# Splitting weights ahead of the two phase changes, rows of tile 1 lagging behind tile 0, gates and reloads of x moved to other queues, and a reordered opening

## The chip, the cores and the metric

The kernel runs on one core of a Trainium2 chip. The metric is the device time of one execution in microseconds (us). TensorE (PE) multiplies, VectorE (DVE) and ScalarE (ACT) do elementwise work, GpSimd (POOL) does a few one-column operations, and SyncE (SP) issues the loads. Each engine works through its own list in order; an instruction that waits holds up everything behind it on its engine.

## The reference

One encoder layer on 256 rows of width 2048 in float32, with three residual steps, each between a modulated norm in front and a gated norm behind:

```python
mod = (c_act @ w_ada[l] + b_ada[l]).reshape(bsz, N_MOD, D_MODEL)[:, :, None, :]
...
h = modulate(rms_norm(x, ffn1_pre_g[l]), sh1, sc1)
y = swiglu(h, ffn1_w_gu[l], ffn1_w_down[l])
x = x + 0.5 * gt1 * rms_norm(y, ffn1_post_g[l])
h = modulate(rms_norm(x, mix_pre_g[l]), sh2, sc2)
proj = h @ w_in[l]
...
y = merged @ w_out[l]
x = x + gt2 * rms_norm(y, mix_post_g[l])
h = modulate(rms_norm(x, ffn2_pre_g[l]), sh3, sc3)
y = swiglu(h, ffn2_w_gu[l], ffn2_w_down[l])
x = x + 0.5 * gt3 * rms_norm(y, ffn2_post_g[l])
```

The middle step turns `proj` into attention heads and a gated block-mixing part, which are normed and joined as `merged`. The hidden width of the two SwiGLU steps is 5504.

## The kernel before

The 256 rows are two tiles of 128, t0 and t1, and the depth of 2048 is 16 blocks of 128 called kt. Every weight is used once for both tiles. Products are made to float32 accuracy with three matmuls of 128x128 by 128x512: the stationary operand and the weight are each split into a coarse part (hi) and a rest (lo), and `mm3` (L106 to L108) adds hi by hi, hi by lo and lo by hi. A weight goes through four steps: a 1 MB load `raw` on SP's queue (L112, three buffers), two casts `hi` on ACT (L144), two subtractions `lo` on DVE (L145), and the matmuls. The pairs `hi`, `lo` stand in slots, 4 from the pool `wsp` and, in some stages, 3 more.

The stages, with the times at which the profiled execution passes them: the opening up to 22 us (norm of x, its transposes `xtp`, the first modulation vectors, and the first split weights); FFN1 up to 747 (gate and up projections `gu`, then down projections `dn`); the in-projections `pj`, attention and gating, up to about 1016; the out-projection `wo` up to 1105; FFN2 up to the end. The modulation vectors come from 144 blocks `ada` of 1 MB, each reduced by one DVE operation (L191) and spread over the program by `tick`, a counter with a rate per visit of a weight.

Two places are called phase changes here. Phase change 1 lies between FFN1's `dn` and the first `pj`, phase change 2 between `wo` and FFN2's first `gu`. At each the kernel has to finish a residual step and begin the next one, for t0 and then for t1: add the last bank of the product to `y` (L428 or L905), square and sum it on ACT (L160), get the reciprocal root `r` with a sum `ms` on DVE (L165) and a power on POOL (L167), multiply by the gate row (L277), update x by `r` (L288, four pieces), square and sum x, get a second `r` in the same way, scale x by it (`xn`, L254), transpose (`xtp`, L257, PE), apply gain and shift while copying out of PSUM (`h`, L264 on ACT and L266 on DVE), and split (`hhi` L244, `hlo` L245). Only then do the matmuls of the next product have an operand.

What stands around that in each engine's list is decided by a scheduler that takes the order of the code, with a higher priority for the phase changes' own steps; `order["split"]` ties the first splits of the next product behind the steps of t0. The first weights of the next product are therefore split among the steps of the change. Inside `in_pair` (L655) and `ffn`, t0 and t1 use each kt in turn; only the second half of `wo` lets t1 lag by 6 kt. The gate row is a column that PE transposes, ACT copies, and two DMAs on SP's queue store to memory (`gd`, L234) and load as a row for all partitions (`gate`, L236). Before phase change 2, x is loaded back from memory on SP's queue (L84).

The opening is written out by hand as two chains, one for ACT and one for DVE (L610 to L616), that are prolonged by the first splits (L474).

## Time and profile before

| | us |
|---|---|
| median of 3 runs | 1850.29 (1850.15 to 1850.95) |
| the profiled execution | 1849.47 |
| its span, first to last instruction | 1847.7 |
| PE busy | 1802.8 |
| DVE busy | 1336.7 |
| ACT busy | 856.2 |
| POOL busy | 29.7 |

The mean granted clock of PE is 0.987 of full speed. A row of the timeline gives start, duration, engine, line, operation and tiles, and in brackets the idle time before it with what ended it. The duration that the profile gives a matmul (0.39 us) is longer than the distance at which matmuls follow each other, since they overlap in the array; a count of starts is the better measure of PE's work. A row of the windows gives, for one stretch, each engine's busy time and instructions, then the granted clock, the busy share of the DMA engines and their GB/s. A row of the waits names who waited for what, the sum, the number of times, and the longest.

### The profile page before, as it was taken

How to read it: one execution, taken by the hardware profiler on the slowest of the kernel's cores; microseconds unless marked ns; L12 is line 12 of the kernel's file. 1: busy time of each engine (PE TensorE's matmuls, PEld its weight loads, DVE VectorE, ACT ScalarE, POOL GpSimd, SP SyncE). 2: the span in 40 equal slices, each digit the busy share in tenths (PEclk: the TensorE clock that was granted, in tenths of full speed). 3: DMA queues.
4: the chain of work that ended last, by engine and by line, in shares of the span. 5: the costliest groups of instructions: out<-in, count | busy, mean ns of one | idle time of the engine just before them, and what ended most of it. 6: DMA issues, size and time to landing. Idle time of an engine off the chain costs nothing. (4 is left out here: it accounts for less than half of the span.)

```text
span 1847.7 us, 21177 instructions
## 1 busy us (share of the span) xinstructions
PE 1802.8 (98%) x8207; PEld 1494.5 (81%) x8207; DVE 1336.7 (72%) x1491; ACT 856.2 (46%) x1105; POOL 29.7 (2%) x54
## 2 busy tenths in 40 slices
PE   7999999999999999899999998999999999999997
PEld 6777788888888898688878876888888888888896
DVE  6989998987878865987889968774445555445455
ACT  6544355454344343745555556444444443443442
POOL 0000000000000000000001100000000000000000
PEclk8999999999999999899999998999999999999999
DMA  8988788988888875588878975885555555555462
GB/s 353 420 335 317 287 321 335 332 330 335 323 325 343 316 275 199 197 326 318 319 300 316 348 278 217 329 320 203 183 187 201 183 193 193 185 199 186 159 247 72
DMA packets 71478, 499.11 MB, mean 270 GB/s; under 512 B 7968, under 2 KB 8144, under 8 KB 13136
## 3 DMA queue, kind: packets, MB, share of 16 engines
q1 hardware_dynamic: 71376, 497.75, 71.6%
q8 instruction: 64, 1.05, 0.2%
q14 instruction: 38, 0.31, 0.0%
HBM read 493.50 MB, written 4.22 MB: 269 GB/s over the span
## 5 line engine op out<-in xcount | busy, mean ns | idle before, releaser
L145 DVE TENSOR_TENSOR lo<-raw,hi 128x1024 fp32r<-128x1024 f32 (+1 forms) x636 | 762.1, 1209 | 444.1 <-ACT hi L144 442.7
L144 ACT CAST hi<-raw 128x1024 fp32r<-128x1024 f32 (+1 forms) x636 | 658.1, 1043 | 883.8 <-PE gu L108 491.4
L106 PE MATMUL gu<-hi,hhi 128*128 128x512 f32 (+1 forms) x1408 | 542.6, 388 | 9.3 <-DVE acc L344 4.2
L107 PE MATMUL gu<-lo,hhi 128*128 128x512 f32 (+1 forms) x1408 | 543.1, 386 | 5.5 <-DVE lo L145 5.5
L108 PE MATMUL gu<-hi,hlo 128*128 128x512 f32 (+1 forms) x1408 | 542.5, 385 | 0.0
L191 DVE CUSTOM_DVE_ANT_0 ada<-ada,c_bc,small 128x2048 f32<-128x2048 f32 x144 | 337.3, 2344 | 9.3 <-DMA ada<-in_w_ada_dram 9.2
L106 PEld LDWEIGHTS gu<-hi,hhi 128*128 128x128 f32 x1408 | 265.6, 189 | 63.4 <-ACT hi L144 5.1
L107 PEld LDWEIGHTS gu<-lo,hhi 128*128 128x128 f32 x1408 | 265.3, 188 | 56.6 <-DVE lo L145 7.3
L108 PEld LDWEIGHTS gu<-hi,hlo 128*128 128x128 f32 x1408 | 265.1, 188 | 50.3 <-DVE hlo L245 0.3
L106 PE MATMUL dn<-hi,ah 128*128 128x512 f32 x640 | 249.2, 389 | 0.0
L107 PE MATMUL dn<-lo,ah 128*128 128x512 f32 x640 | 249.0, 389 | 0.0
L108 PE MATMUL dn<-hi,al 128*128 128x512 f32 x640 | 249.0, 389 | 0.0
L106 PEld LDWEIGHTS dn<-hi,ah 128*128 128x128 f32 x640 | 120.1, 188 | 25.0
L107 PEld LDWEIGHTS dn<-lo,ah 128*128 128x128 f32 x640 | 120.2, 188 | 24.9
L108 PEld LDWEIGHTS dn<-hi,al 128*128 128x128 f32 x640 | 120.1, 188 | 24.9
L107 PE MATMUL pj<-lo,hhi 128*128 128x512 f32 x320 | 127.7, 399 | 5.5 <-DVE lo L145 5.4
L106 PE MATMUL pj<-hi,hhi 128*128 128x512 f32 x320 | 128.2, 401 | 0.4 <-ACT hhi L244 0.4
L108 PE MATMUL pj<-hi,hlo 128*128 128x512 f32 x320 | 127.1, 398 | 0.0
L107 PEld LDWEIGHTS pj<-lo,hhi 128*128 128x128 f32 x320 | 60.7, 190 | 18.7 <-DVE lo L145 7.6
L106 PEld LDWEIGHTS pj<-hi,hhi 128*128 128x128 f32 x320 | 60.8, 190 | 12.3 <-ACT hhi L244 0.9
L108 PEld LDWEIGHTS pj<-hi,hlo 128*128 128x128 f32 x320 | 60.7, 190 | 11.6
L167 POOL TENSOR_TENSOR r<-ms,mhalf 128x1 f32<-128x1 f32 x16 | 21.4, 1335 | 1583.5 <-DVE ms L165 1583.5
(145 smaller groups left out, 1014.2 us busy)
## 6 DMA issues: line engine op xcount, KB each, us to landing
raw<-in_w_gu_dram SPq DMA_DIRECT2D x158, 1024.0 KB, 4.8
ada<-in_w_ada_dram SPq DMA_DIRECT2D x144, 1024.0 KB, 6.9
raw<-in_w_dn_dram SPq DMA_DIRECT2D x86, 1024.0 KB, 4.8
raw<-in_w_in_dram SPq DMA_DIRECT2D x40, 1024.0 KB, 5.0
raw<-in_w_out_dram SPq DMA_DIRECT2D x16, 1024.0 KB, 4.9
raw<-in_w_gu_dram SPq DMA_DIRECT2D x16, 768.0 KB, 4.3
x<-in_x_dram SPq DMA_DIRECT2D x4, 1024.0 KB, 7.4
...
```

What stands on the lines that cost most here:

```text
L106: nc.tensor.matmul(ps, ah, wh, start=start, stop=False)
L107: nc.tensor.matmul(ps, ah, wl, start=False, stop=False)
L108: nc.tensor.matmul(ps, al, wh, start=False, stop=stop)
L144: i_hi = nc.scalar.copy(hi[:, :n], raw)
L145: i_lo = nc.vector.tensor_tensor(lo[:, :n], raw, hi[:, :n].bitcast(F32), op=ALU.subtract)
L167: nc.gpsimd.tensor_tensor(r, ms, mhalf, op=ALU.pow)
L191: inst = nc.vector.tensor_tensor_reduce(out=st, in0=st, in1=c_bc, scale=1.0, scalar=bada[:, i:i + 1], op0=ALU.mult, op1=ALU.add, accum_out ...
```

## The change

The number of large matmuls stays, and so do the loads of weights. Seven things are new.

- **Splits ahead at phase change 1.** `down_last` calls `ahead1` after its own weights: three visits of `w_in` (6 kt) are loaded and split before t0's last banks are read out, into slots that now also come from the two `ada` buffers and a new pool. `in_pair(sp=sp1, lag=8)` uses them; t0 runs ahead, and t1 follows 8 kt behind.
- **Splits ahead at phase change 2.** The first three visits of FFN2's `w_gu2` are loaded and split in the second half of `wo` (one half-visit after it), and FFN2's first chunk is a `lead_chunk` with the same lag of 8. The second half of `wo` no longer lags by 6: t0 does kt 0 to 3 and then bank by bank kt 4 to 7, and t1 the same after it.
- **The scaling of x by `r`.** In `pre`, the four DVE operations `xn` of 128x512 per tile are gone. One DVE operation makes `dg`, the identity times `r`, and PE multiplies x by `dg` in plain float32 where it transposed `xn`.
- **Gates and reloads of x.** The store `gd` goes on ACT's queue and the load `gate` on GpSimd's, and both are put off by two ticks; the reload of x before phase change 2 goes on GpSimd's queue, earlier. The second gate is made inside the last `out_pair`.
- **The opening.** Both tiles' sums of squares are shared between ACT and DVE; three of four copies of `c_bc` are on ACT; of t1's four scalings one is on DVE; and the cast `hi` of the second weight stands ahead of three late copies of `xnT`.
- **Slots** are taken from sequences that `use_slots` writes down for each stage.
- **The rate** of `ada` blocks in FFN1 is 0.77 instead of 0.7.

The core of the diff:

```diff
+    def use_slots(*parts, once=()):
+        flat = lambda ps: [p for p, n in ps for _ in range(n)]
+        slots["seq"] = itertools.chain(flat(once), itertools.cycle(flat(parts)))
+    def slot():
+        pool = next(slots["seq"])
+        if pool is adap:
+            st = adap.tile([P, D], F32R, tag="ada", name=nm("adas"))
+            return st[:, :1024], st[:, 1024:]
...
+        if later:
+            step = later.pop(0)
+            if step:
+                step()
...
-        row = sm.tile([KT, P], F32, tag="xn", name=nm("grow"), bufs=2)
-        nc.scalar.copy(row, ps)
-        gd = dr.tile([KT, P], F32, tag=f"gd{i}", name=nm("gd"))
-        nc.sync.dma_start(gd, row)
-        g = gp.tile([P, D], F32, tag="gate", name=nm("gate"))
-        nc.sync.dma_start(g, gd[:, :].rearrange("k p -> (k p)").partition_broadcast(P))
-        return g
+        res = []
+        def spread():
+            row = sm.tile([KT, P], F32, tag="xn", name=nm("grow"), bufs=2)
+            inst = nc.scalar.copy(row, ps)
+            after(inst, order["last"][0])
+            gd = dr.tile([KT, P], F32, tag=f"gd{i}", name=nm("gd"))
+            nc.scalar.dma_start(gd, row)
+            g = gp.tile([P, D], F32, tag="gate", name=nm("gate"))
+            nc.gpsimd.dma_start(g, gd[:, :].rearrange("k p -> (k p)").partition_broadcast(P))
+            res.append(g)
+        later.extend([None, spread])
+        return res
...
+        dg = sm.tile([P, P], F32, tag="xn", name=nm("dg"), bufs=2)
+        nc.vector.tensor_scalar(dg, ident, r, None, op0=ALU.mult)
         for j in range(4):
-            xn = sm.tile([P, CH], F32, tag="xn", name=nm("xn"), bufs=2)
-            nc.vector.tensor_scalar(xn, x[t][:, j * CH:(j + 1) * CH], r, None, op0=ALU.mult)
             ps = ptr.tile([P, 4, P], F32, tag="tr", name=nm("xtp"))
             for q in range(4):
-                nc.tensor.transpose(ps[:, q, :], xn[:, q * P:(q + 1) * P], ident)
+                nc.tensor.matmul(ps[:, q, :], x[t][:, (4 * j + q) * P:(4 * j + q + 1) * P], dg, start=True, stop=True)
...
+        def lead_chunk(c, sp):
+            w = CHUNKS[c][1]
+            ps_of[c] = banks()
+            sp = list(sp)
+            def mm(kt, t):
+                for b in range(2):
+                    mv = (sp[kt][0][:, b * w:(b + 1) * w], sp[kt][1][:, b * w:(b + 1) * w])
+                    mm3(ps_of[c][b][t][:, :w], hst(kt, t), mv, kt == 0, kt == KT - 1)
+            for kt in range(KT + LEAD):
+                if kt < KT and kt >= len(sp):
+                    raw = gu_load(c, kt // 2)
+                    sp += [split(raw[:, 2 * q * w:2 * (q + 1) * w]) for q in range(2)]
+                if kt < KT:
+                    mm(kt, 0)
+                if kt >= LEAD:
+                    mm(kt - LEAD, 1)
...
+            if not tail:
+                ahead()
...
-            chain(first_act, hi0, h0[0], h0[1], late_evac[0], late_evac[1], late_evac[2], hi1, hi2, h1[0], h1[1], hi3)
+            chain(first_act, hi0, h0[0], h0[1], hi1, late_evac[0], late_evac[1], late_evac[2], hi2, h1[0], h1[1], hi3)
...
+            if lead and c == 0:
+                lead_chunk(0, lead)
+                use_slots(*after_lead)
+                p0 = pe
...
-    xn1 = on_act[-4:]
-    first_act = chain(*on_act[:-4], xn1[0], xn1[1], i_evac[0, 0], i_evac[0, 1], xn1[2], xn1[3],
-                      i_evac[0, 2], i_evac[0, 3], i_evac[1, 0])
+    first_act = chain(i_silu, sq_act[0], *i_c[1:], sq_act[1], i_evac[0, 0], i_evac[0, 1],
+                      i_xn[1, 1], i_xn[1, 2], i_xn[1, 3], i_evac[0, 2], i_evac[0, 3], i_evac[1, 0])
     late_evac = [i_evac[1, j] for j in range(1, 4)]
-    first_dve = chain(*on_dve)
+    first_dve = chain(i_c[0], sq_dve[0], i_ms[0], i_xn[0, 0], i_xn[0, 1], sq_dve[1], i_ms[1],
+                      i_xn[0, 2], i_xn[0, 3], i_xn[1, 0])
...
+        def ahead1():
+            ahs.close()
+            pre = wx.enter_context(tc.tile_pool(name="pre1", bufs=2))
+            rest = ((adap, 2), (pre, 2), (wsp, 4), (wx1, 3))
+            use_slots(*rest, once=((wx1, 1),) + rest)
+            for _ in range(3):
+                sp1.extend(in_visit())
...
-        ffn(a["w_gu1"], a["w_dn1"], h, ap_, PLAN, 0.7, gate1, finish1)
+        ffn(a["w_gu1"], a["w_dn1"], h, avp, ahp, PLAN, 0.77, gate1, finish1, ahead=ahead1)
...
+        for kt in range(KT + lag):
+            if kt < KT and kt >= len(sp):
+                sp += in_visit()
+            for b in range(2):
+                if kt < KT:
+                    mm(kt, 0, b)
+                if kt >= lag:
+                    mm(kt - lag, 1, b)
...
-    pa = in_pair()
+    pa = in_pair(sp=sp1, lag=LEAD)
     tick_acc[1] = 0.9
-    slots["extra"] = None
+    use_slots((wsp, 1))
...
+        def gate2():
+            flush_ada(GT[1])
+            gain(2, 0, KT)
+            g.append(gate(1, 1.0, gp))
+        ps = out_pair(m_b, [gate2])
...
+        use_slots((adap, 1), once=((wsp, 3), (wx2, 3), (wsp, 1)))
+        sp = wo_visit() + wo_visit()
         for t in range(NT):
             for b in range(2):
-                evac_b(t, b, ps[b][t])
-        LAG = 6
+                evac_b(t, b, ps[b][t], order["last"])
+        x2.extend(load_x(x_dram, nc.gpsimd))
         ps = wo_banks()
-        sp = []
-        for kt in range(8 + LAG):
-            if kt < 8 and kt % 2 == 0:
-                sp += wo_visit()
-            if kt < 8:
-                wo_mm(ps, m_b, sp[kt], kt, 0)
-            if kt >= LAG:
-                wo_mm(ps, m_b, sp[kt - LAG], kt - LAG, 1)
+        for kt in range(4):
+            wo_mm(ps, m_b, sp[kt], kt, 0)
+        sp += wo_visit() + wo_visit()
+        for b in range(2):
+            for kt in range(4, 8):
+                wo_mm(ps, m_b, sp[kt], kt, 0, (b,))
+        use_slots((wsp, 1), once=((adap, 1), (wsp, 4)))
+        sp3 = []
+        for p in range(3):
+            raw = load(a["w_gu2"], p * P * 2048, 2048)
+            sp3.append((raw, [split(raw[:, 1024 * q:1024 * (q + 1)]) for q in range(2 if p < 2 else 1)]))
+        for kt in range(4):
+            wo_mm(ps, m_b, sp[kt], kt, 1)
+        for b in range(2):
+            for kt in range(4, 8):
+                wo_mm(ps, m_b, sp[kt], kt, 1, (b,))
...
+        lead = [sl for _, sls in sp3 for sl in sls] + [split(raw[:, 1024:])]
```

On DVE at phase change 1, before (`y_395` and `y_396` are t0's and t1's sums, `dn_5559` t0's last bank, `dn_5577` to `dn_5597` t1's first three, `ms_5572` and `ms_5633` the two sums of squares of t0):

```order
L428 TENSOR_TENSOR y_395_2045<-y_395_2045,dn_5559 128x512
L165 TENSOR_REDUCE ms_5572<-ysq_5483 128x1
L277 TENSOR_TENSOR y_395_2045<-y_395_2045,gate_5177 128x512
L288 SCALAR_TENSOR_TENSOR x_969_5162<-y_395_2045,r_5574,x_969_5162 128x512 x4
L428 TENSOR_TENSOR y_396_2046<-y_396_2046,dn_5577 128x512
L428 TENSOR_TENSOR y_396_2046<-y_396_2046,dn_5587 128x512
L165 TENSOR_REDUCE ms_5633<-xsq_5619 128x1
L428 TENSOR_TENSOR y_396_2046<-y_396_2046,dn_5597 128x512
L254 TENSOR_SCALAR xn_5637<-x_969_5162,r_5635 128x512
```

and now, with `y_392` and `y_393` for t0 and t1, `dn_5610` t0's last bank and `dn_5628` to `dn_5648` t1's first three:

```order
L479 TENSOR_TENSOR y_392_2049<-y_392_2049,dn_5610 128x512
L479 TENSOR_TENSOR y_393_2050<-y_393_2050,dn_5628 128x512
L176 TENSOR_REDUCE ms_5623<-ysq_5502 128x1
L303 TENSOR_TENSOR y_392_2049<-y_392_2049,gate_5234 128x512
L314 SCALAR_TENSOR_TENSOR x_972_5184<-y_392_2049,r_5625,x_972_5184 128x512 x4
L303 TENSOR_TENSOR y_393_2050<-y_393_2050,gate_5234 128x512
L479 TENSOR_TENSOR y_393_2050<-y_393_2050,dn_5638 128x512
L479 TENSOR_TENSOR y_393_2050<-y_393_2050,dn_5648 128x512
L176 TENSOR_REDUCE ms_5684<-xsq_5670 128x1
L156 TENSOR_TENSOR lo_5543<-raw_5540,hi_5542 128x1024
L277 TENSOR_SCALAR dg_5688<-ident,r_5686 128x128
```

The add of t1's first bank stands ahead of t0's first `ms` where it stood behind the updates of x; a gate multiplication of t1 and two adds stand ahead of the second `ms`, and a split of weights (`lo_5543`) between it and `dg`, where the first `xn` was.

On PE at the same place, before, from t0's third group of transposes (`waits` names the engines whose signal an instruction waits for):

```order
L257 MATMUL xtp_5667<-ident,xn_5665 128x128 [waits DVE_49,Activation_49]
L257 MATMUL xtp_5667<-ident,xn_5665 128x128 x3
L106 MATMUL pj_5791<-hi_5797,hhi_5617 128x512 [waits Activation_49]
L257 MATMUL xtp_5681<-ident,xn_5679 128x128 [waits DVE_49,Activation_49]
L257 MATMUL xtp_5681<-ident,xn_5679 128x128 x3
L107 MATMUL pj_5791<-lo_5798,hhi_5617 128x512 [waits DVE_49]
L108 MATMUL pj_5791<-hi_5797,hlo_5618 128x512
L106 MATMUL pj_5791<-hi_5813,hhi_5617 128x512
L107 MATMUL pj_5791<-lo_5814,hhi_5617 128x512 [waits DVE_49]
L108 MATMUL pj_5791<-hi_5813,hlo_5618 128x512
```

and now:

```order
L281 MATMUL xtp_5714<-dg_5688,x_972_5184 128x128 [waits DVE_49,Activation_49]
L281 MATMUL xtp_5714<-dg_5688,x_972_5184 128x128 x3
L113 MATMUL pj_5828<-hi_5542,hhi_5668 128x512 [waits Activation_49]
L114 MATMUL pj_5828<-lo_5543,hhi_5668 128x512
L113 MATMUL pj_5830<-hi_5542,hhi_5668 128x512
L114 MATMUL pj_5830<-lo_5543,hhi_5668 128x512
L281 MATMUL xtp_5726<-dg_5688,x_972_5184 128x128 [waits DVE_49,Activation_49]
L281 MATMUL xtp_5726<-dg_5688,x_972_5184 128x128 x3
L115 MATMUL pj_5828<-hi_5542,hlo_5669 128x512 [waits DVE_49]
L115 MATMUL pj_5830<-hi_5542,hlo_5669 128x512
L113 MATMUL pj_5828<-adas_5546,hhi_5668 128x512
L114 MATMUL pj_5828<-adas_5546,hhi_5668 128x512
```

Each `lo` used to carry a wait for DVE; now the waits on this stretch are for `hhi`, `hlo` and the copies out of PSUM, and the weights of the next kt (`adas_5546`) carry none.

On PE at phase change 2, before, from t0's third group of transposes:

```order
L257 MATMUL xtp_8686<-ident,xn_8684 128x128 [waits DVE_49,Activation_49]
L257 MATMUL xtp_8686<-ident,xn_8684 128x128 x3
L106 MATMUL wo_8487<-hi_8560,mb_7491 128x512
L107 MATMUL wo_8487<-lo_8561,mb_7491 128x512
L108 MATMUL wo_8487<-hi_8560,mb_7492 128x512
L106 MATMUL gu_8810<-hi_8816,hhi_8624 128x512 [waits Activation_49]
L257 MATMUL xtp_8700<-ident,xn_8698 128x128 [waits DVE_49,Activation_49]
L257 MATMUL xtp_8700<-ident,xn_8698 128x128 x3
L107 MATMUL gu_8810<-lo_8817,hhi_8624 128x512
L108 MATMUL gu_8810<-hi_8816,hlo_8625 128x512 [waits DVE_49]
L106 MATMUL gu_8810<-hi_8820,hhi_8624 128x512
L107 MATMUL gu_8810<-lo_8821,hhi_8624 128x512
```

and now, from the last matmul of `wo`:

```order
L115 MATMUL wo_8512<-adas_8553,mb_7500 128x512
L281 MATMUL xtp_8687<-dg_8685,x_1657_8505 128x128 [waits DMASW1_49,DVE_49]
L281 MATMUL xtp_8687<-dg_8685,x_1657_8505 128x128 x3
L281 MATMUL xtp_8699<-dg_8685,x_1657_8505 128x128 x4
L281 MATMUL xtp_8711<-dg_8685,x_1657_8505 128x128 [waits DVE_49,Activation_49]
L281 MATMUL xtp_8711<-dg_8685,x_1657_8505 128x128 x3
L113 MATMUL gu_8834<-adas_8582,hhi_8653 128x512 [waits Activation_49]
L114 MATMUL gu_8834<-adas_8582,hhi_8653 128x512
L113 MATMUL gu_8836<-adas_8582,hhi_8653 128x512
L281 MATMUL xtp_8723<-dg_8685,x_1657_8505 128x128 [waits DVE_49,Activation_49]
L281 MATMUL xtp_8723<-dg_8685,x_1657_8505 128x128 x3
L115 MATMUL gu_8834<-adas_8582,hlo_8654 128x512 [waits DVE_49]
```

Matmuls of `wo` for t1 used to stand between the groups of transposes; now they all stand ahead of the first one.

On ACT in the opening, before:

```order
L160 ACTIVATE junk_144,xsq_153<-x_2_91 128x2048
L600 ACTIVATE xn_188<-x_2_91,r_158 128x512
L600 ACTIVATE xn_195<-x_2_91,r_158 128x512
L611 COPY xnT_216<-xtp_162 128x4x128
L611 COPY xnT_216<-xtp_169 128x4x128
L600 ACTIVATE xn_202<-x_2_91,r_158 128x512
L600 ACTIVATE xn_209<-x_2_91,r_158 128x512
L611 COPY xnT_217<-xtp_176 128x4x128
L611 COPY xnT_217<-xtp_183 128x4x128
L611 COPY xnT_216<-xtp_190 128x4x128
L144 CAST hi_239<-raw_226 128x1024
L625 ACTIVATE h_42_243<-xnT_216,mod,gmul 128x256
```

and now:

```order
L171 ACTIVATE junk_144,xsq_153<-x_2_91 128x1024
L667 COPY xnT_214<-xtp_164 128x4x128
L667 COPY xnT_214<-xtp_171 128x4x128
L656 ACTIVATE xn_18_161<-x_2_91,r_159 128x512 x3
L667 COPY xnT_215<-xtp_178 128x4x128
L667 COPY xnT_215<-xtp_185 128x4x128
L667 COPY xnT_214<-xtp_191 128x4x128
L155 CAST hi_237<-raw_224 128x1024
L681 ACTIVATE h_39_241<-xnT_214,mod,gmul 128x256
L268 CAST hhi_112<-h_39_241 128x256
L155 CAST hi_245<-raw_226 128x1024
L667 COPY xnT_214<-xtp_197 128x4x128
```

The square of x's second tile covers half the width, one of four scalings (`xn`) is gone from the list, the first `xnT` copies stand ahead of the scalings, and the second weight's cast (`hi_245`, before `hi_247`) follows `hhi` directly, ahead of three copies.

More of the change, by code (lines that the diff above doesn't have):

```diff
@@ L627, in h_first, with in_visit @@
         return (i_h,) + split_act(h32, h[0][:, kt, :], h[1][:, kt, :])
+    win_off = [0]
+    def in_visit():
+        raw = load(a["w_in"], win_off[0], 2048)
+        win_off[0] += P * 2048
+        tick()
+        return [split(raw[:, 1024 * q:1024 * (q + 1)]) for q in range(2)]
     PLAN = []
@@ L913, in block_kernel @@
-        ps = out_pair(m_b)
-        x2.extend(load_x(x_dram))
+            inst = nc.vector.scalar_tensor_tensor(out=y[t][:, ns], in0=ps, scalar=rb[t], in1=y[t][:, ns], op0=ALU.mult, op1=ALU.add)
+            if behind:
+                after(inst, behind[1])
+            return y_done(t, n, y, ysq, g, sm.tile([P, CH], F32, tag="xn", name=nm("junk"), bufs=2), behind)
+        use_slots((wsp, 4), (wx2, 3))
+        g = []
+        def gate2():
+            flush_ada(GT[1])
+            gain(2, 0, KT)
+            g.append(gate(1, 1.0, gp))
```

156 lines of the change are left out of this document (79 added, 77 removed).

## The prediction

> **What bounds the kernel now.** I read the page's engine rows and its groups first, then PE's timeline where it waits.
>
> ```profile
> PE 1802.8 (98%) x8207; PEld 1494.5 (81%) x8207; DVE 1336.7 (72%) x1491; ACT 856.2 (46%) x1105; POOL 29.7 (2%) x54
> ```
>
> ```profile
> L145 DVE TENSOR_TENSOR lo<-raw,hi 128x1024 fp32r<-128x1024 f32 (+1 forms) x636 | 762.1, 1209 | 444.1 <-ACT hi L144 442.7
> ```
>
> PE is busy for 98% of the span, and the large matmuls stay as many, so a gain can only come from the stretches where PE waits or runs at a lower clock. DVE splits the weights in 636 operations of 1.21 us, and PE's two longest waits after the opening are for such a `lo`. The timeline of PE shows them, first at phase change 1, then at phase change 2:
>
> ```profile
> 746.93 1.06 PE L257 MATMUL xtp<-ident,xn 128*128 128x128 f32 x8 [0.42 <-DVE xn L254]
> 749.95 0.66 PE L257 MATMUL xtp<-ident,xn 128*128 128x128 f32 x4 [1.95 <-ACT h L264]
> ...
> 759.63 0.80 PE L107 MATMUL pj<-lo,hhi 128*128 128x512 f32 x1 [5.17 <-DVE lo L145]
> ```
>
> ```profile
> 1106.91 1.09 PE L257 MATMUL xtp<-ident,xn 128*128 128x128 f32 x8 [1.45 <-DVE xn L254]
> 1107.76 0.48 PE L108 MATMUL wo<-hi,mb 128*128 128x512 f32 x1
> ...
> 1122.19 0.80 PE L107 MATMUL gu<-lo,hhi 128*128 128x512 f32 x1 [3.51 <-DVE lo L145]
> ```
>
> What each change costs in all is a count. Eight transposes take 0.85 us (1106.91 to 1107.76), 0.106 each. The distance of large matmuls is read in `wo`, beside a product in plain float32 (`zp`) that I need below:
>
> ```profile
> 1021.00 1.95 PE L844 MATMUL zp<-uv,wst 128*128 128x128 f32 x16
> 1022.70 0.48 PE L106 MATMUL wo<-hi,ma 128*128 128x512 f32 x1
> ...
> 1023.25 0.39 PE L108 MATMUL wo<-hi,ma 128*128 128x512 f32 x1
> ...
> 1028.01 0.39 PE L108 MATMUL wo<-hi,ma 128*128 128x512 f32 x1
> ```
>
> From 1023.25 to 1028.01 there are 21 steps, 0.227 each. Now the windows that hold the two changes, for PE whole, and for `xtp` alone:
>
> ```profile
> 746.10:769.30 23.20, 14.61 (x56) 9.59 (x55) 21.77 (x39) 19.80 (x46) 2.56 (x5) 0.71 0.42 163
> 1105.00:1128.80 23.80, 14.78 (x65) 10.68 (x64) 21.47 (x37) 20.02 (x44) 2.92 (x4) 0.78 0.30 111
> ```
>
> ```profile
> 746.10:769.30 23.20, 5.87 (x32) 4.49 (x32) 2.67 (x7) 7.07 (x18) 0.71 0.42 163
> 1105.00:1128.80 23.80, 4.92 (x28) 3.84 (x28) 2.34 (x6) 6.90 (x18) 0.78 0.30 111
> ```
>
> Phase change 1 holds 56 - 32 = 24 large matmuls and 32 transposes: 24 x 0.227 + 32 x 0.106 = 8.8 us of work in 23.2, a loss of 14.4. Phase change 2 holds 37 and 28: 11.4 of 23.8, a loss of 12.4. Part of the loss is clock, 0.71 and 0.78 on average:
>
> ```profile
> 748.20:751.60 3.40, 1.24 (x6) 0.69 (x7) 3.40 (x9) 3.40 (x9) 0.00 (x0) 1.00 0.00 0
> 1113.40:1116.80 3.40, 0.90 (x3) 0.30 (x2) 3.38 (x7) 3.40 (x12) 0.10 (x1) 1.00 0.49 207
> 215.70:219.10 3.40, 1.60 (x6) 1.05 (x6) 3.40 (x6) 1.27 (x2) 0.00 (x0) 1.00 0.44 183
> 752.00:765.00 13.00, 7.53 (x21) 4.72 (x20) 12.12 (x20) 9.93 (x22) 2.39 (x4) 0.50 0.45 166
> ```
>
> After 3.4 us with PE busy for 1.24, the clock was 0.50 for 13 us; after 0.90 it fell as well; after 1.60 it did not.
>
> **Phase change 1.** The splits ahead remove the wait of 5.17 us and those after it: kt 0 to 5 are split before, and 6 kt of t0 alone are 36 matmuls, 8.2 us of work that needs no split. What is late next is the chain to the second `r`. Its old course on DVE:
>
> ```profile
> 738.81 0.68 DVE L428 TENSOR_TENSOR y<-y,dn 128x512 f32<-128x512 f32 x1
> 740.34 0.16 DVE L165 TENSOR_REDUCE ms<-ysq 128x1 f32<-128x5 f32 x1 [0.85 <-ACT junk L160]
> ...
> 745.39 0.15 DVE L165 TENSOR_REDUCE ms<-xsq 128x1 f32<-128x5 f32 x1
> 745.46 0.68 DVE L428 TENSOR_TENSOR y<-y,dn 128x512 f32<-128x512 f32 x1
> 746.30 0.88 DVE L254 TENSOR_SCALAR xn<-x,r 128x512 f32<-128x512 f32 x2 [0.16 <-POOL r L167]
> ```
>
> An ACT cast of the splits ahead now stands before the cast of `aw` and waits for PE; I put 0.55 us of idle PE on it, about half a cast (2.01 for two in a row quoted below; bounds 0 and 1.1). The add of t1's first bank moves ahead of t0's first `ms`. That bank ends 9 matmuls, 2.04 us, after t0's last, so with the 0.55 the add ends near 742.0 where `ms` began at 740.34: the chain is 1.7 us later. The updates follow as before, but a gate multiplication (as long as the add, 0.68) comes ahead of the second `ms`, which so begins at 745.39 + 1.7 + 0.68 = 747.8, and a split of 1.2 us and the end of POOL's power stand between `ms` and `dg`. That gives `dg` at 749.5 against the end of `dn` at 746.93 - 0.42 + 0.55 = 747.05, and PE idle for 2.1 to 2.7 us where it was 0.42; I take 2.4, the middle. The third group of products waits until the first is copied out: 1.95 above, and less now that no cast stands ahead of that copy on ACT, so between 0 and 1.95; I take 0.75. The first `pj` waits for `hhi` and the first `hlo` product again, 0.45 together by the 0.20 to 0.25 that one signal takes. Then t1: DVE has 21 operations between the two `dg`, about 14 us at 0.4 to 1.2 each with two POOL waits, and PE 16 products and 36 matmuls, 11.6 us, and the 1.2 us of waits just named; I get 1.0 (0 to 2). Sum of idle: 0.55 + 2.4 + 0.75 + 0.45 + 1.0 = 5.15.
>
> The products with `dg` are plain float32 matmuls. The 16 records of `zp` are 8 products in 1.70 us, 0.213 each: 32 x (0.213 - 0.106) = 3.4 us of PE more. The four removed `xn` save DVE 1.8 us per tile, which lie beside other work. So the loss becomes 8.55 instead of 14.4: **5.85 gained**.
>
> **Phase change 2.** `wo` for t1 now ends before the first product, and the chain's last add, that of t1's final bank, stands ahead of `dg` and waits for PE's last `wo`. That add (some 0.7), POOL's power, `dg` and the signals between them make PE wait 1.6 to 2.4 us where it waited 1.45 and then had `wo` to do; I take 2.1, nearer to the upper end, since a cast stands ahead of the last squares on ACT. The copy of the first group costs 1.1, since a split stands ahead of it on DVE, `hhi` 0.2, t1's `dg` 1.2 (0 to 2). That is 4.6, and 3.4 for float32: 8.0 instead of 12.4, **4.4 gained**.
>
> **The opening.**
>
> ```profile
> 21.80 1.22 PE L106 MATMUL gu<-hi,hhi 128*128 128x512 f32 x2 [2.15 <-ACT hhi L244]
> 31.16 0.50 PE L106 MATMUL gu<-hi,hhi 128*128 128x512 f32 x1 [0.76 <-ACT hhi L244]
> ```
>
> ```profile
> 23.09 2.01 ACT L144 CAST hi<-raw 128x1024 fp32r<-128x1024 f32 x2
> 30.07 0.60 ACT L625 ACTIVATE h<-xnT,mod,gmul 128x256 f32<-128x256 f32 x1 [4.96 <-DVE gmul L203]
> ```
>
> ```profile
> 20.00:30.00 10.00, 8.20 (x23) 6.50 (x24) 7.37 (x9) 5.07 (x8) 0.00 (x0) 0.60 0.83 347
> 30.00:40.00 10.00, 9.24 (x41) 7.25 (x40) 9.44 (x11) 8.40 (x13) 0.00 (x0) 1.00 0.79 304
> 60.00:70.00 10.00, 10.00 (x45) 7.94 (x43) 9.96 (x11) 5.18 (x8) 0.00 (x0) 1.00 1.02 428
> ```
>
> Adding up ACT's list in its new order, `hhi` comes near 17 to 18 instead of 21.8, about 4 us earlier; the second cast (23.09) stands in front of the late copies, so the second pair of `ada` and with it the next `h` (30.07) come 5 to 6 us earlier. But the loads are the limit soon after: the DMA engines are full at 60 to 70, and what they have free is 0.17 and 0.21 of two windows, 3.8 us. I take **3.5 gained** (1.5 to 5.5). The rate of 0.77 moves `ada` blocks to where DVE still has idle time, and I cost it at nothing.
>
> **Sum.** 5.85 + 4.4 + 3.5 = 13.75 from 1849.47 gives 1835.7; the runs' median lies 0.8 above the profiled execution, so 1836.5.
>
> **Gate and clock, against the Trainium skill.**
>
> ```profile
> L167 POOL TENSOR_TENSOR r<-ms,mhalf x16: 550/928/2591, 9.0 to 1840.0; 128x1 f32<-128x1 f32 x16
> ```
>
> ```profile
> DMA to landing us min/median/max: 6.8/7.4/8.2
> ```
>
> The second gate is the tight one. It is put off to the third of four visits of the last `out_pair`, 2 x 24 x 0.227 = 10.9 us into it. Splits run about a visit (5.4) ahead of PE; with 7.4 us for the load and as much again for the store before it, it lands at 10.9 - 5.4 + 14.8 = 20.3. It is needed when the pair (21.8 us) and four adds are done, at 24.5: some 4 us to spare. The reload of x goes out ahead of it on the same queue and is needed a half `wo` later (24 x 2 x 0.227 = 10.9 us), and gates 1 and 3 have a whole `dn` between load and use; with that cover I cost them at nothing, and without it they would stop DVE in the same way. The slots only say where a split is kept: at nothing too, as long as no split waits for a slot that PE still reads, and then for at most that kt's 12 matmuls, 2.7 us. In these rows a one-column POOL operation takes 0.55 us at best and 2.59 beside a busy DVE, 4.7 times as long.
> The Trainium skill (SBUF — State Buffer, "SBUF: two separate sides") says that a DMA from GpSimd's queue has its descriptors written by GpSimd, which some VectorE operations lock out; a 620 ns transfer became 3100, and by that factor of 5 the estimate for this gate is 37 us. The rows of POOL agree in kind; no load on that queue is in this trace.
>
> On the clock, the skill (TensorE: Matmul & The Clock Gate, "HAM oscillation") has the abstract rule "no PE-idle gaps >~3.4µs". By it the longest new gap, 2.7, would keep the clock, and the first rival below would have no chance. The trace differs: the longest single gap in the 3.4 us before 751.6 was 1.95, and the clock fell, so the rows decide.
>
> **The rivals.**
> - *The clock falls again* at one or both changes. A gap of 2.1 to 2.4 leaves PE at most 1.3 of 3.4 us if it lies within one such stretch (between 1.24, which fell, and 1.60, which did not), more if it is shared by two. Two to three stretches at half clock cost 3.4 to 5.1: 1840 for one, 1844 for both. Chance 0.27.
> - *The opening is hidden* by full DMA engines: 1836.5 + 3 = 1839.5. For it speaks 1.02 at 60 to 70. Chance 0.09.
> - *The phases gain little*, because the chain to `dg`, and not the splits, sets them: t1's `dg` comes 3 us later at each, 1842.5 for both. For it speaks how many operations remain between; chance 0.08.
> - *Slower: the second gate lands late.* DVE stops at the first multiplication, and behind it in its list stand all splits of the second half of `wo`, so PE stops too. At 7.4 x 4.7 = 35 us it is 27.6 later, less 4 to spare: 1836.5 + 23.4 = 1860. The change turns slower from a load of about 26 us on. Against it: POOL does little else, and only the issuing could stretch. Chance 0.06.
>
> The forecast itself has 0.50. If every gap is at its lower bound (0.55 + 0.3 + 0.75 + 1.0 less at the first change, 0.5 + 1.2 at the second) and the opening gives 5.5, it is 1830.2; with one fall of the clock at 5.1 and an opening of 1.5 it is 1843.6. The range, rounded outward, is 1829 to 1844. About 0.2% (3.7 us) is what a measurement can tell from no change: all cases but the last lie below 1846.6, and I leave 0.06 for two falls of the clock together with a poor opening. Faster 0.88, same 0.06, slower 0.06.
>
> **What would show it.** Right: no wait of PE for `lo` at either change, one gap of 2 to 3 us ahead of each first `xtp`, product records at 0.106 two by two, the clock at 1.00 through both, the first `gu` near 18. Wrong: a clock of 0.50 after a change; DVE waiting for the gate's DMA; a long gap before t1's products; PE waiting for `hi` or `lo` between 30 and 90.

## The result, and the profile after

The changed kernel takes 1839.39 us (median of 4 runs, 1838.25 to 1840.22) where the kernel before, run beside it, takes 1850.62. The ratio is 0.9935, with a 95% interval from 0.9923 to 0.9946: 11 us faster. The forecast was 1836.5, in a range of 1829 to 1844. The profiled execution took 1839.32 us, 10.15 less than the one of before, with a span of 1837.2. One execution of experiment eight took 2600.89 us at a granted clock of 0.654, a slow state, and is not in its median below.

The page's row of the engines, and two rows of PE's waits (sum, number, longest):

```profile
PE 1803.2 (98%) x8271; PEld 1501.1 (82%) x8271; DVE 1328.4 (72%) x1481; ACT 854.5 (47%) x1105; POOL 31.3 (2%) x59
```

```profile
PE dn L113 <- ACT aw L424: 1.1, 2, 0.9
...
PE gu L114 <- DVE lo L156: 0.3, 1, 0.3
```

PE has 64 records more (8271 against 8207), the second halves of the 64 products with `dg`. Its waits for `lo`, which held the two longest before, are down to one of 0.3 us, in the opening. PE's timeline at phase change 1, then at phase change 2:

```profile
748.30 4.73 PE L281 MATMUL xtp<-dg,x 128*128 128x128 f32 x24 [2.30 <-issue]
...
763.09 2.02 PE L281 MATMUL xtp<-dg,x 128*128 128x128 f32 x16 [0.81 <-ACT hi L155]
```

```profile
1104.32 2.05 PE L281 MATMUL xtp<-dg,x 128*128 128x128 f32 x16 [1.77 <-DVE dg L277]
1107.57 1.16 PE L281 MATMUL xtp<-dg,x 128*128 128x128 f32 x8 [1.20 <-ACT h L288]
...
1116.59 2.02 PE L281 MATMUL xtp<-dg,x 128*128 128x128 f32 x16 [0.58 <-ACT hi L155]
```

One gap stands ahead of each first product, 2.30 and 1.77 us, and short ones later. The row of the first names no releaser; DVE's timeline has it:

```profile
746.19 0.15 DVE L176 TENSOR_REDUCE ms<-xsq 128x1 f32<-128x5 f32 x1
746.26 1.21 DVE L156 TENSOR_TENSOR lo<-raw,hi 128x1024 fp32r<-128x1024 f32 x1
747.91 0.28 DVE L277 TENSOR_SCALAR dg<-ident,r 128x128 f32<-128x128 f32 x1 [0.44 <-POOL r L178]
```

A split of 1.21 us stands between the second sum and `dg`, as the prediction had it, and `dg` ends at 748.19, 0.1 before the first product. The count that the prediction made of before is made here again: windows around the two changes, for PE whole, then for `xtp` alone.

```profile
745.60:769.50 23.90, 20.79 (x115) 17.63 (x113) 19.39 (x34) 19.51 (x45) 3.00 (x6) 0.93 0.56 215
1102.10:1123.60 21.50, 17.95 (x109) 15.24 (x109) 19.99 (x34) 21.01 (x48) 2.08 (x4) 1.00 0.46 160
```

```profile
745.60:769.50 23.90, 9.85 (x64) 9.20 (x64) 2.77 (x7) 7.58 (x20) 0.93 0.56 215
1102.10:1123.60 21.50, 8.39 (x64) 7.78 (x64) 2.85 (x7) 7.93 (x21) 1.00 0.46 160
```

Phase change 1 holds 115 - 64 = 51 large matmuls and 64 records of products: 51 x 0.227 + 64 x 0.106 = 18.4 us of work in 23.9, 5.5 lost. The second halves of the products, 32 x 0.106 = 3.4, are work that before did not have, and ahead of the window PE waits for `aw`, 1.1 us in all where the waits of before have 0.5:

```profile
PE dn L106 <- ACT aw L376: 0.5, 2, 0.2
```

That is 5.5 + 3.4 + 0.6 = 9.5 against 14.4 of before: 4.9 gained. Phase change 2 holds 45 and 64: 17.0 of 21.5, 4.5 lost, 7.9 with the 3.4, against 12.4: 4.5 gained. The clock at phase change 1:

```profile
745.40:748.80 3.40, 1.10 (x7) 0.71 (x6) 2.96 (x7) 3.17 (x7) 1.42 (x2) 0.99 0.79 304
748.80:752.20 3.40, 3.40 (x17) 3.12 (x16) 2.12 (x6) 1.90 (x7) 0.00 (x0) 0.51 0.75 294
752.20:755.60 3.40, 3.40 (x24) 2.90 (x23) 3.40 (x7) 3.09 (x7) 0.97 (x2) 1.00 0.00 0
```

After 3.4 us with PE busy for 1.10, the clock is halved for one stretch of 3.4 us: 1.7 us lost. At phase change 2 it stays at 1.00, as the row of that window above has it.

**The opening.** PE's timeline, ACT's list just before PE's last wait there, and the windows of after; then the same windows of before.

```profile
18.24 1.21 PE L113 MATMUL gu<-hi,hhi 128*128 128x512 f32 x2 [2.31 <-ACT hhi L268]
...
50.95 1.20 PE L113 MATMUL gu<-hi,hhi 128*128 128x512 f32 x4 [1.62 <-ACT hi L155]
```

```profile
46.42 1.08 ACT L388 COPY acc<-gu 128x512 f32<-128x512 f32 x2 [1.23 <-PE gu L115]
...
49.37 0.59 ACT L388 COPY acc<-gu 128x512 f32<-128x512 f32 x1 [0.77 <-PE gu L115]
49.85 2.00 ACT L155 CAST hi<-raw 128x1024 fp32r<-128x1024 f32 x2
```

```profile
0.00:40.00 40.00, 31.34 (x133) 26.19 (x134) 28.81 (x36) 25.92 (x42) 2.37 (x19) 0.96 0.95 390
40.00:80.00 40.00, 37.76 (x156) 29.55 (x155) 36.34 (x40) 24.48 (x37) 0.00 (x0) 0.96 0.97 398
80.00:120.00 40.00, 39.03 (x171) 31.45 (x170) 35.80 (x41) 15.84 (x18) 0.00 (x0) 1.00 0.88 342
```

```profile
0.00:40.00 40.00, 28.23 (x111) 22.61 (x112) 26.03 (x33) 24.64 (x39) 4.24 (x19) 0.79 0.86 342
40.00:80.00 40.00, 39.44 (x173) 31.75 (x172) 36.88 (x40) 25.32 (x38) 0.00 (x0) 1.00 1.01 426
80.00:120.00 40.00, 39.03 (x171) 31.46 (x170) 35.83 (x42) 16.73 (x20) 0.00 (x0) 1.00 0.90 348
```

The first `gu` comes at 18.24 instead of 21.80, and at 40 us PE has started 22 matmuls more than before. At 80 us the lead is 5, and it stays 5 up to 120: 5 x 0.227 = 1.1 us is what is left. The rows of ACT show a place where it goes. Copies of finished banks stand ahead of two casts and wait for PE again and again; PE then waits 1.62 us for these casts. From 40 to 80 us the loads ran at a share of 0.97 and 398 GB/s, where before has 1.01 and 426, so they alone do not explain it.

4.9 + 4.5 + 1.1 make 10.5, which is the whole difference of the two spans (1847.7 and 1837.2).

### The profile page after: what moved, and what is told of

The parts are those of the page before. It is cut to its first block, busy times and chain, and to the rows that moved or that the text cites. A ratio compares the mean times of both kernels' runs of the same rounds, so it can differ in the third digit from the quotient of the medians.

```text
span 1837.2 us, 21286 instructions
## 1 busy us (share of the span) xinstructions
PE 1803.2 (98%) x8271; PEld 1501.1 (82%) x8271; DVE 1328.4 (72%) x1481; ACT 854.5 (47%) x1105; POOL 31.3 (2%) x59
## 4 chain that ended last, share of the span: by engine, by line
PE 93%; DVE 4%; ACT 1%; issue 1%; DMA 0%; POOL 0%; POOLq 0%; DVEq 0%; SPq 0%; ACTq 0%
PE gu L114 16%; PE gu L115 16%; PE gu L113 16%; PE dn L113 8%; PE dn L114 8%; PE dn L115 8%; PE pj L113 4%; PE pj L115 4%; PE pj L114 4%; PE wo L113 1%; PE wo L115 1%; PE wo L114 1%; DVE lo L156 1%; PE atp L418 1%; PE xtp L281 1%
## 5 line engine op out<-in xcount | busy, mean ns | idle before, releaser
L155 ACT CAST hi<-raw 128x1024 fp32r<-128x1024 f32 (+1 forms) x628 | 645.9, 1042 | 811.5 <-PE gu L115 422.6
L156 DVE TENSOR_TENSOR lo<-raw,hi 128x1024 fp32r<-128x1024 f32 (+1 forms) x628 | 747.8, 1208 | 380.9 <-ACT hi L155 379.5
L113 PE MATMUL gu<-hi,hhi 128*128 128x512 f32 (+1 forms) x1396 | 536.8, 387 | 8.9 <-DVE acc L392 4.2
L113 PE MATMUL pj<-hi,hhi 128*128 128x512 f32 x304 | 120.9, 398 | 0.0
L114 PE MATMUL pj<-lo,hhi 128*128 128x512 f32 x304 | 120.4, 396 | 0.0
L115 PE MATMUL pj<-hi,hlo 128*128 128x512 f32 x304 | 120.1, 395 | 0.0
L453 DVE TENSOR_TENSOR y<-y,dn 128x512 f32<-128x512 f32 x64 | 41.9, 682 | 17.5 <-PE dn L115 17.5
```

What stands on the lines that cost most here:

```text
L113: nc.tensor.matmul(ps, ah, wh, start=start, stop=False)
L114: nc.tensor.matmul(ps, ah, wl, start=False, stop=False)
L115: nc.tensor.matmul(ps, al, wh, start=False, stop=stop)
L155: i_hi = nc.scalar.copy(hi[:, :n], raw)
L156: i_lo = nc.vector.tensor_tensor(lo[:, :n], raw, hi[:, :n].bitcast(F32), op=ALU.subtract)
L453: nc.vector.tensor_tensor(y[t][:, ns], y[t][:, ns], ps[t], op=ALU.add)
```

## The experiments

All times are medians, with before run beside each. What is set against the changed kernel is 1839.39 us, ratio 0.9935. The kernel before took between 1850.62 and 1852.29 beside the different runs, so where a us or two matters, the ratios to before are compared too.

**One: the scaling of x as before.** `xn` and the transposes come back in `pre`; all else is as changed.

```diff
-        dg = sm.tile([P, P], F32, tag="xn", name=nm("dg"), bufs=2)
-        nc.vector.tensor_scalar(dg, ident, r, None, op0=ALU.mult)
         for j in range(4):
+            xn = sm.tile([P, CH], F32, tag="xn", name=nm("xn"), bufs=2)
+            nc.vector.tensor_scalar(xn, x[t][:, j * CH:(j + 1) * CH], r, None, op0=ALU.mult)
...
-                nc.tensor.matmul(ps[:, q, :], x[t][...], dg, start=True, stop=True)
+                nc.tensor.transpose(ps[:, q, :], xn[:, q * P:(q + 1) * P], ident)
```

> The changed kernel with the four scalings xn on DVE and the transposes of before in place of dg and the float32 products. Theory A (the products cost PE 0.107 us more each, 3.4 us at each phase change, and the chain on DVE gains little by dg): 4 to 6 us faster than the changed kernel, near 1834. Rival B (the four xn of 0.44 us are on DVE's chain at both tiles, and the wait for t1 grows by what they take): no faster, 1839 to 1842.

It takes 1833.66 us (1833.50 to 1834.57), ratio 0.9907 [0.9893, 0.9920]: 5.7 us faster than the change. Theory A holds: the plain float32 products are the part of the change that costs. By the count they cost 2 x 3.4 = 6.8. What comes back against that is seen in PE's timeline and in the clock, at phase change 1 and, in the last row, at phase change 2:

```profile
748.58 1.45 PE L281 MATMUL xtp<-ident,xn 128*128 128x128 f32 x8 [2.54 <-DVE xn L278]
751.02 1.08 PE L281 MATMUL xtp<-ident,xn 128*128 128x128 f32 x4 [0.99 <-ACT h L288]
```

```profile
748.80:752.20 3.40, 2.41 (x13) 1.90 (x12) 3.08 (x8) 2.58 (x8) 0.00 (x0) 0.55 0.67 275
752.20:755.60 3.40, 3.40 (x11) 2.71 (x11) 3.40 (x8) 3.40 (x7) 0.01 (x1) 0.50 0.02 5
...
1104.10:1107.51 3.41, 3.28 (x11) 2.65 (x12) 3.41 (x5) 3.41 (x11) 0.00 (x0) 0.50 0.31 82
```

The gap before the first transposes is hardly longer than with `dg` (2.54 against 2.30), so the fewer DVE operations bought 0.2 us there. The third group waits 0.99 for a copy, which the longer products covered, and the clock stays low for two stretches where it was one. At phase change 2 it falls for one stretch too, where it stayed up in the change. The net gain is therefore unequal: from 740 to 1090 us PE starts 14 large matmuls more than in the change (3.2 us), and from 1090 to 1130 nine more (2.0 us).

**Two: the opening as before**, with its two hand-written chains; all else as changed.

```diff
-            chain(first_act, hi0, h0[0], h0[1], hi1, late_evac[0], late_evac[1], late_evac[2], hi2, h1[0], h1[1], hi3)
+            chain(first_act, hi0, h0[0], h0[1], late_evac[0], late_evac[1], late_evac[2], hi1, hi2, h1[0], h1[1], hi3)
...
-    first_dve = chain(i_c[0], sq_dve[0], i_ms[0], i_xn[0, 0], i_xn[0, 1], sq_dve[1], i_ms[1],
-                      i_xn[0, 2], i_xn[0, 3], i_xn[1, 0])
+    first_dve = chain(*on_dve)
```

> The changed kernel with the opening of before. Theory A (the opening's 4.8 us are given back between 40 and 56 us, where PE waits for casts and the clock halves once): within 1.5 us of the changed kernel, 1839 to 1841, with first gu near 21.8 and no wait of PE between 40 and 56. Rival B (the forecast: the opening is worth 3.5 us): 1843.

1840.22 us (1839.51 to 1842.01), ratio 0.9943 [0.9929, 0.9957]: 0.8 us slower than the change. By the time, theory A holds and rival B does not. The opening that I sized at 3.5 is worth 0.8 by the medians and 1.5 by the ratios; by 120 us PE has started 453 matmuls here and 460 in the change, 1.6 us.

**Three: the copies behind the next visit's casts.** If the copies of finished banks hold up the casts, they can be tied behind them on ACT.

```diff
-                        nc.scalar.copy(acc[c][b][t], ps_of[c][b][t])
+                        after(nc.scalar.copy(acc[c][b][t], ps_of[c][b][t]), order["last"][0])
```

> The changed kernel with each copy of a spilled bank on ACT placed behind the casts of the next weight. Theory A (ACT's list holds copies that wait for PE ahead of casts whose raw landed 6 us earlier): the wait of PE for hi near 49 us and the lower clock after it go, 3 us faster, near 1836. Rival B (DMA engines full from 20 to 70 us set the pace): ACT's casts wait for raw instead and PE waits as long, 1838 to 1840. Rival C (the copies then free PSUM banks late): PE waits for banks, slower than 1840.

1855.29 us (1851.17 to 1857.04), ratio 1.0018 [1.0009, 1.0027]: slower even than before. Rival C came true. The casts so moved ahead belong to the visit after the one now due; they wait for a slot that PE still reads (the first row, of ACT: 422.6 us in the change), with the copies behind them, and PE waits for the banks (the other):

```profile
ACT hi L155 <- PE gu L115: 502.6, 282, 8.9
```

```profile
PE gu L113 <- ACT acc L388: 9.8, 5, 2.2
```

By 120 us PE has started 391 matmuls where the change has 460: 69 x 0.227 = 15.7 us, nearly the whole loss. This settled nothing on whether the copies cost anything where they stand; experiment five does.

**Four: no lag of t1 at phase change 1.** The splits ahead stay; t0 and t1 use each kt in turn.

```diff
-    pa = in_pair(sp=sp1, lag=LEAD)
+    pa = in_pair(sp=sp1)
```

> The changed kernel with t1 not lagging in the first in-projection; the splits ahead stay. Theory A (t1's operand is ready some 16 us after dn ends, and PE must have t0's work until then): if t1's kt 0 is called for earlier, PE waits longer; some 3 to 8 us slower than the changed kernel. Rival B (the scheduler puts t0's first bank ahead by itself, and 6 kt of one bank, then later weights, fill part of the time): within 2 us.

1840.67 us (1840.10 to 1842.65), ratio 0.9946 [0.9932, 0.9959]: 1.3 us slower, so rival B holds by the total. It does not hold at phase change 1 alone: from 740 to 1090 us PE starts 12 large matmuls fewer than in the change, 2.7 us, with a wait of 0.50 us for `lo` among the causes. Phase change 2 gives 6 matmuls back (1.4 us, with a first gap of 0.84 instead of 1.77), from another order there, in which some of t1's `wo` products stand among those with `dg`; why, was not looked into. So the scheduler replaces the lag only in part.

**Five: the copies behind the casts of the visit now due.** This starts from experiment one, and ties the copies one visit earlier than experiment three.

```diff
-        def spill(c):
+        def spill(c, now=None):
...
-                        nc.scalar.copy(acc[c][b][t], ps_of[c][b][t])
+                        inst = nc.scalar.copy(acc[c][b][t], ps_of[c][b][t])
+                        if now:
+                            after(inst, now)
...
+                now = order["last"][0]
                 prep(v + 1)
...
-                        spill(o)
+                        spill(o, now)
```

> The changed kernel with `xn` and transposes instead of `dg` products (that alone took 1833.7 us), and with each copy of a finished bank placed on ACT behind the casts of the visit now due, not of the next one. Theory A (the early gain of the opening is lost because casts stand on ACT behind copies that wait for PE): the wait of PE for hi near 49 us goes, DVE has no idle time there, and the time is 2 to 3 us shorter, near 1831. Rival B (loads and VectorE limit the stretch up to 70 us whatever ACT does): PE waits later, near 60 to 70, for hi or lo by as much, and the time stays within 1 us of 1833.7. Rival C (the copies come too late, PE waits for the banks): slower, over 1835.

1830.76 us (1829.94 to 1831.59), ratio 0.9885 [0.9872, 0.9899]: 2.9 us under experiment one, and theory A holds. Its windows, to be read beside those of after:

```profile
0.00:40.00 40.00, 29.95 (x128) 24.98 (x129) 29.73 (x37) 26.45 (x43) 2.36 (x19) 0.87 0.96 391
40.00:80.00 40.00, 39.86 (x176) 32.75 (x175) 39.49 (x42) 25.48 (x38) 0.00 (x0) 1.00 1.01 427
80.00:120.00 40.00, 38.55 (x169) 31.28 (x169) 35.40 (x42) 15.84 (x18) 0.00 (x0) 1.00 0.88 342
```

PE is busy for 39.86 of the 40 us between 40 and 80, and by 120 it has started 473 matmuls where the change has 460, experiment one 459 and before 455: 18 x 0.227 = 4.1 us ahead of before. The loads run fuller than in the change (1.01 and 427 GB/s against 0.97 and 398), and PE does not wait for them. So it was the order on ACT, and not the loads, that took the opening's gain back.

**Six: the first `lo` of the splits ahead moved back.** In the change, this operation of 1.21 us stands between the second `ms` and `dg` at phase change 1. Here, again with `xn`, it is tied behind t0's second `xn`.

```diff
+            i_xn = nc.vector.tensor_scalar(xn, x[t][...], r, None, op0=ALU.mult)
+            if j == 1 and order.get("first"):
+                after(order.pop("first"), i_xn)
...
+            sp1.append(split(raw[:, :1024]))
+            order["first"] = order["last"][1]
```

> The changed kernel with `xn` and transposes instead of `dg` products (1833.7 us), and with the rest (lo) of the first weight split ahead at phase change 1 placed on VectorE behind t0's second `xn`, not ahead of the chain's end. Theory A (that operation of 1.2 us stands in the chain to the first product): PE's gap before the first transposes falls from 2.5 to about 1.4 us, 1 us shorter in all, and 1.7 us more if the clock then stays up after it: 1831 to 1833. Rival B (the first `pj` now waits for that lo, or the gap is POOL's and ACT's): no change within 0.7 us of 1833.7.

1840.08 us (1839.69 to 1841.59), ratio 0.9939 [0.9925, 0.9953]: 6.4 us slower than experiment one. The gap fell as theory A said, and more came back, where neither theory had its size. PE's and DVE's timelines:

```profile
747.66 1.06 PE L283 MATMUL xtp<-ident,xn 128*128 128x128 f32 x8 [1.73 <-DVE xn L278]
...
757.44 0.80 PE L114 MATMUL pj<-lo,hhi 128*128 128x512 f32 x1 [3.95 <-DVE lo L156]
```

```profile
756.17 1.22 DVE L156 TENSOR_TENSOR lo<-raw,hi 128x1024 fp32r<-128x1024 f32 x1
```

The tie sets the earliest place; the scheduler then put every step of the phase change, which has the higher priority, ahead of it, up to 756.17. The first product with it waited 3.95 us, at half clock; rival B had named this wait. The splits ahead are worth their place only if none is late.

**Seven and nine: gates and x back on SP's queue.** Seven takes both back, nine only the reload of x.

```diff
-            nc.scalar.dma_start(gd, row)
+            nc.sync.dma_start(gd, row)
...
-            nc.gpsimd.dma_start(g, gd[:, :].rearrange("k p -> (k p)").partition_broadcast(P))
+            nc.sync.dma_start(g, gd[:, :].rearrange("k p -> (k p)").partition_broadcast(P))
...
-        x2.extend(load_x(x_dram, nc.gpsimd))
+        x2.extend(load_x(x_dram))
```

> The changed kernel with the stores and loads of the gates and the reload of x back on SP's queue; all else as changed (1839.4 us). Theory A (the queues of ScalarE and GpSimd hide these transfers and so did SP's): within 1 us of 1839.4. Rival B (a load on GpSimd's queue is held up or disturbs VectorE): 2 to 5 us faster. Rival C (on SP's queue the gate stands behind loads of weights that wait for buffers, and DVE waits for it at a residual step): slower by 2 us or more, with DVE waiting for the gate's DMA.

> The changed kernel with only the reload of x ahead of phase change 2 back on SP's queue; the gates stay on the queues of ScalarE and GpSimd. With both back the time was 1843.3 us where the change alone takes 1839.4. Theory A (two loads of 1 MB of x stand ahead of the last weights of `wo` on SP's queue, so the scheduler puts t1's products ahead of t0's last ones and t0's last bank ends late): PE's gap before the first products of phase change 2 grows from 1.8 to about 6.5 us and the time is near 1843. Rival B (it is the gate's store and load on SP's queue that move the order): within 1 us of 1839.4.

Seven takes 1843.34 us (1842.85 to 1844.86), ratio 0.9955 [0.9941, 0.9968], 4.0 slower; nine 1841.89 (1841.47 to 1843.89), ratio 0.9949 [0.9935, 0.9964], 2.5 slower. The loss is at phase change 2 in both. PE's first product there in seven, then in nine, with DVE's wait ahead of it:

```profile
1108.51 5.73 PE L281 MATMUL xtp<-dg,x 128*128 128x128 f32 x24 [6.50 <-DVE dg L277]
```

```profile
1106.45 5.49 PE L281 MATMUL xtp<-dg,x 128*128 128x128 f32 x24 [5.16 <-DVE dg L277]
```

```profile
1094.98 1.43 DVE L983 SCALAR_TENSOR_TENSOR y<-wo,r,y 128x512 f32<-128x512 f32 x2 [6.34 <-PE wo L115]
```

DVE does not wait for a DMA, as rival C of seven had it, but for PE. Of t1's 48 products in the second half of `wo`, 12 stand ahead of t0's last one in the change's order, 23 in nine's and 29 in seven's. That makes t0's last banks, and with them the chain to `dg`, later by 11 x 0.227 = 2.5 us in nine and by 17 x 0.227 = 3.9 in seven, which happens to be near the losses in time. It is not all of them, since the clock falls at phase change 2 in both and stayed up in the change; in nine:

```profile
1104.00:1112.00 8.00, 5.42 (x25) 5.09 (x26) 7.44 (x14) 4.81 (x13) 2.44 (x3) 0.57 0.73 263
```

From 1090 to 1130 us PE starts 174 matmuls in nine and 168 in seven where the change has 191: 3.9 and 5.2 us. Nine has some 1 us of it back from phase change 1, where its clock stays up. The last two weights of `wo` do land later with the loads of x ahead of them. Their size and median us from issue to landing, in after and then in nine:

```profile
raw<-in_w_out_dram SPq DMA_DIRECT2D x2, 1024.0 KB, 7.5
```

```profile
raw<-in_w_out_dram SPq DMA_DIRECT2D x2, 1024.0 KB, 12.6
```

PE does not wait for them in either run: in nine its order has t1's products to do first. The scheduler fixes that order beforehand by what it reckons, and it seems to reckon these weights late; that this reckoning is the link is argued from the order, not shown. So theory A of nine holds in kind (a gap of 5.16 where it put 6.5) and has the larger part, 2.5 of 4.0; the gates have the rest.

**Eight: no splits ahead at phase change 1.** Slots and lag stay.

```diff
-            for _ in range(3):
-                sp1.extend(in_visit())
```

> The changed kernel without the three visits of the in-projection's weight that are split ahead at phase change 1; slots, lag and all else as changed (1839.4 us). Theory A (the splits ahead carry the gain of phase change 1): PE waits for `lo` again behind the first `pj`, 3.5 us or more in all, and the time is 4 to 6 us longer, 1843.4 to 1845.4. Rival B (lag and slots alone let the scheduler split as early): within 1 us of 1839.4. Rival C (without the splits the chain to `dg` is shorter by as much as the first splits then cost): within 2 us, with a gap before the first products of 1 us or less.

1843.40 us (1842.44 to 1845.16), ratio 0.9955 [0.9940, 0.9970]: 4.0 slower by the medians, 3.7 by the ratios. Theory A holds, with part of rival C in it:

```profile
745.14 2.02 PE L281 MATMUL xtp<-dg,x 128*128 128x128 f32 x16 [0.19 <-issue]
...
757.99 0.50 PE L114 MATMUL pj<-adas,hhi 128*128 128x512 f32 x1 [4.37 <-DVE adas L156]
```

Without the splits ahead the first gap is 0.19 instead of 2.30, and the wait for a `lo` is back, 4.37 us. So they are worth about 4 us net, after paying 2.1 for the longer chain.

**Ten: the first `lo` ahead of the second `ms`.** This starts from experiment five (1830.76 us). The `lo` is put ahead of the sum, beside ACT's squares, and t1's gate multiplication and adds behind it, beside GpSimd's power.

```diff
+        if order.get("first"):
+            after(order["first"], order["split"][-1][1])
+            after(order["mean"], order.pop("first"))
+            order["hold"] = order["mean"]
...
-                nc.vector.tensor_tensor(y[t][:, ns], y[t][:, ns], ps, op=ALU.add)
+                inst = nc.vector.tensor_tensor(y[t][:, ns], y[t][:, ns], ps, op=ALU.add)
+                if n and order.get("hold"):
+                    after(inst, order["hold"])
```

> The kernel with `xn` and with the copies of finished banks behind the casts of the visit now due (1830.8 us), and at phase change 1 with the first weight's rest (lo) ahead of the second sum of squares on VectorE, and t1's gate multiplications and adds behind that sum; each is then beside the wait for ScalarE's squares or for the power on GpSimd. Theory A (lo and t1's two adds stand in the chain to the first product): the sum comes 0.7 us earlier, PE's gap before the first transposes falls from 2.5 to 1.2 us or less, and the time by 1 to 3 us, 1828 to 1830. Rival B (t1's adds are missed later: t1's second `r` comes later and PE waits there by as much): within 0.7 us of 1830.8.

1829.96 us (1828.93 to 1830.47), ratio 0.9882 [0.9865, 0.9898]: 0.8 under experiment five, 0.9885 [0.9872, 0.9899]. The medians lean to theory A, the intervals overlap nearly whole, and so it stays open. PE's timeline shows why so little came of it:

```profile
743.34 1.06 PE L285 MATMUL xtp<-ident,xn 128*128 128x128 f32 x8 [1.35 <-DVE xn L282]
746.04 1.12 PE L285 MATMUL xtp<-ident,xn 128*128 128x128 f32 x4 [1.64 <-ACT h L292]
```

```profile
744.00:748.00 4.00, 2.36 (x11) 1.79 (x10) 3.97 (x9) 3.78 (x11) 0.00 (x0) 0.66 0.69 262
```

The first gap is down to 1.35, but the copy of the first group still makes the third wait, 1.64, and the two waits lie in the same few microseconds, so the clock falls as before. With 1829.96 this is the fastest kernel that was run: 22 us under before and 9.4 under the change.

## Why the prediction was right, and where it was not

- **Phase change 1, forecast 5.85, measured 4.9.** The mechanism was right: no wait for `lo` is left, and what is late next is the chain to `dg`. The gaps came out near what was put or shorter: 0.6 for `aw` (0.55), 2.30 ahead of the first product (2.4), none ahead of the third group (0.75), 0.81 for t1 (1.0). What the sum did not hold is the clock: the rival "the clock falls again" came true here, for one stretch, at 1.7 us. I had priced it at 3.4 to 5.1 for two or three stretches, from the 13 us of before; with split weights at hand PE is busy right after the gap, and the clock came back after one. That it fell at all was partly chance: in experiment nine the same gap of 2.30 us left it up (last section).
- **Phase change 2, forecast 4.4, measured 4.5.** The gap ahead of the first product is 1.77 (2.1), the copy 1.20 (1.1), t1's wait 0.58 (1.2), and the clock stays up, as forecast. Both rest in part on luck. The order of PE's products that makes the gap 1.77 came with the new queues: on SP's queue it is 6.50 (experiment seven), which no term of the sum held. And the gap, from 1102.55 to 1104.32, is shared by two of the clock's stretches of 3.41 us, which meet at 1103.73 (last section); with `xn`, where the waits here are 1.96 and 1.95, the clock fell (experiment one).
- **The products with `dg`, forecast 6.8 us of cost.** Right in the count of records, and taking them out gains 5.7 (experiment one). What they were to buy on DVE does not shorten the chain.
- **The opening, forecast 3.5, measured 1.1 by the count and 0.8 by the medians (experiment two).** This is the term that was mis-sized. That the first `hhi` comes 4 us earlier was right, and at 40 us the lead was 22 matmuls. The step that failed is the next one, "the loads are the limit soon after": I read the DMA share as the only bound and did not go through ACT's list behind the first casts. There the copies of finished banks wait for PE ahead of casts, and with the casts of the due visit ahead of them (experiment five) 13 matmuls, 3.0 us, stay, and the loads run fuller than in the change. The rival "the opening is hidden by full DMA engines" therefore has nearly the right time, 1839.5, for the wrong reason and by luck, since its sum has no fall of the clock in it.
- **Gates, reload of x, slots, at nothing.** Wrong for the queues: with these transfers back on SP's queue the kernel is 4.0 us slower (experiment seven), 2.5 of it with the reload alone (nine). I had asked only whether these loads arrive in time, not what their place on SP's queue does to the order of PE's products. Phase change 2's 4.5 stands on this: seven loses 5.2 there. The slots, and the rate of 0.77, were not tried by themselves.
- **The second gate late** did not happen, but the margin was not the 4 us that I reckoned. The rows of the gate's tile (time to landing), of the gate's load and of DVE's first use:

```profile
DMA to landing us min/median/max: 6.6/8.4/9.5
```

```profile
1071.43 0.53 POOL L257 DMA_DIRECT2D gate<-gd  x1 [32.47 <-issue]
```

```profile
1081.55 2.49 DVE L303 TENSOR_TENSOR y<-y,gate 128x512 f32<-128x512 f32 x4
```

  This load took 9.5 us and landed at 1080.9, 0.6 ahead of its use. On SP's queue the three took 6.8 to 8.2 before, and 6.1 to 6.8 in experiment seven. The Trainium skill (SBUF — State Buffer, "SBUF: two separate sides") has a DMA of GpSimd's queue starve while VectorE holds the port, by a factor of 5 in its example. The trace bears that out at most by a little: 8.4 against 7.4 (before) and 6.3 (seven) at the median, with VectorE busy for 72% of the span.

Of the forecast 13.75 us, 10.5 came by the spans: the opening fell short by 2.4 and the clock took 1.7, and the shorter gaps gave about 0.8 back. The measured 1839.39 lies in the stated range, but nearer to what two rivals gave (1839.5 and 1840) than to the forecast's 1836.5.

## What to carry to other kernels

A gain at the start is worth what the next stage lets through: go on down each engine's list past the first saving, and look for instructions that wait for the engine that was sped up. Splitting ahead removes a wait for data and lengthens the chain beside it, so find what is late next and keep out of that chain each operation that no one waits for; but tie it with a latest place, not only an earliest one. When a scheduler orders the work, moving a load to another queue can move matmuls too, so compare the order of the bound engine, not only the arrival of the loads.
